# One issue in GpSimd's queue two operations later: the third sum of w_o blocks

## The chip, the cores and the metric

The kernel runs on one core of a Trainium2 chip. The metric is device time in microseconds of one execution. Every comparison is made against runs of the kernel before on the same chip. TensorE is called PE, VectorE DVE, ScalarE ACT, GpSimd POOL or G, and SyncE, which issues most transfers, SP.

## The reference

One decoder layer on x of shape (1, 512, 1024) in float32:

```python
h = x @ w_in                       # q, six k/v streams, gates, GDN q/k/v, beta, decay, merge gates
y_a = nsa_attention(...) @ w_nsa_out   # 8 heads of 64: compressed, selected and window branches
y_b = gated_deltanet(...) @ w_gdn_out  # 4 heads of 128: conv, chunked WY form, gated RMS norm
mix = (sigmoid(gate_a) * y_a + sigmoid(gate_b) * y_b) @ w_o
x = layer_norm(alpha * x + mix)
x = layer_norm(alpha * x + conv_ffn(x))    # (silu(gate) * val) @ w_down, gate and val through a width-3 conv
```

The DeltaNet inverts, for each head and chunk, a lower triangular matrix I + m. The products with `w_o` and `w_down` are what the sums of weight blocks below are for.

## The kernel before, in words

Each float32 product is made of three PE products of rounded parts: a tile `raw` is loaded, `wh` is its rounded copy (line 467 on ACT, 469 on DVE or GpSimd) and `wl = raw - wh` (line 471, on DVE or GpSimd, as a table says for each tile). PE then multiplies wh with the high and the low part of the other operand (lines 481 and 483, out is `gps` in the input projection) and wl with the high part (484).

The two output products, with `w_o` and `w_down`, are done as a seven-product scheme on 2x2 blocks, which needs sums of weight blocks. Those sums are made in DRAM by transfers that GpSimd issues, some of them adding (`accum_op`). For `w_o` they are the eight transfers of `sums_o`, written into `osum[0]` to `osum[3]`; nothing reads the finished sums before the product with `w_o`, some 390 us into the kernel (line 1168):

```python
todo = [(0, o[0, :, 0], 0), (1, o[0, :, 1], 0), (0, o[0, :, 1], 1), (1, o[1, :, 1], 1), (2, osum[1], 0), (2, o[0, :, 0], 1),
        (3, osum[2], 0), (3, o[1, :, 0], 1)]
for to, src, add in todo:
    G.dma_start(out=osum[to], in_=src, **({"accum_op": OP.add} if add else {}))
```

So `osum[2]` is first copied from `osum[1]`, then w_o's block (0, 0) is added to it, and `osum[3]` is copied from it later.

The order of every engine's instructions is written out: the table QUEUES has for each engine the numbers of its instructions (in the order in which the program makes them) in the order in which they are to run, and `queues` chains them with order-only dependencies. In the row of the table for Pool, 104 to 111 are the eight transfers of `sums_o`; 109 is the sixth, the adding transfer into `osum[2]`.

The place of the change lies where the DeltaNet of the third head is inverted while attention heads and the input projection run on PE beside it. The names there:

- `z` (line 772, GpSimd): the start of the inverse, made from `xs`, a DVE recursion of small steps (769, 770).
- `at` (line 740, GpSimd): a mask on the chunk's q-k products. It is used later, in `gdn_out` (line 861).
- CAST `wh` (469) and `wl` (471) on GpSimd: the first half of an input-projection tile, which PE takes up after the tile in work.
- `ym` (line 787, DVE) and line 790 on PE: a step of the inverse, `gdn_inv`:

```python
        PE.matmul(py[:, c, :], m[:, c, :], half(z)[:, c], start=True, stop=True)          # 785
    V.tensor_tensor(ym, py, bc(C["m16"][:, None, 0:64], (128, TT, 64)), op=OP.mult)       # 787
    ...
        PE.matmul(pz[:, c, :], x[:, c, :], ym[:, c, :], start=True, stop=True)            # 790
```

- `kh` and `kl` (907, ACT; 909, DVE): the two parts of the keys of the second group, which the scores (1039, 1040 on PE) need; the mask and exponent of the scores are lines 1043 and 1045.
- 656 and 1072 are PE transposes, 1086 and 1092 products of attention.

Of the kernel before, what the change touches and what calls it, by code (L numbers as in the profile page):

```python
# [70 lines left out]
def layout(a):  # L71
# [251 lines left out]
760-763 756 765-766 753 768-769 772 771 773-774 770 767 764 775 777 776 778-788 790 789 792 791 794 793 796 795  # L323
797-798""",
    "Pool": """2 1 0 8 10 9 11-12 3 13 4-6 15 7 16-17 19 141 20-22 27-28 105 33 23 25 18 34 29 39 38 30-31 43 32 14 44 40 107 24 35
37 140 62 26 41 45 54 48 55 42 36 49 51 47 52 64 66 65 67 46 68 57 69 58 50 53 56 59 61 108 104 63 109 75 60 76 80 88
77 81 87 90 110 78 71 84 72-73 70 93 85 74 92 94 86 82 91 95 111 144 96-97 83 98-99 79 100 106 101-102 89 103 112-130
132 131 133-137 147 150 138-139 142-143 145 153 148 146 149 151-152 154-155 157 156 158-161 163 162 165 164 166-171""",
    "SP": """0-7 17 8-9 15 25 10 12 11 13-14 19 18 16 20-24 26-75 80 79 81-82 78 83 77 84-85 76 86-134 136-165 167 135 169 171
# [1239 lines left out]
```

## Time and profile before

| what | value |
|---|---|
| runs | 825.55, 825.56, 827.45 us; median 825.56 |
| profiled execution | 824.98 us, with a span of 823.2 us |
| mean granted TensorE clock | 0.994 |
| PE busy | 804.0 us of the span |
| GpSimd busy | 179.5 us of the span, 176 instructions |
| adding and plain `osum` loads from w_o | 6 of 1024 KB, median 9.1 us from issue to landing |

The page shows one execution. Busy times are sums over the span; the chain of work that ended last is followed back from the last instruction to what released it. Rows of the order of time have the start in us, the duration in us, the engine, the line, the operation, what is written and read, and in square brackets the idle time of the engine ahead of it with what ended that. An engine's instructions are in order, so a wait at the head of a queue holds all behind it. Issues of transfers are not counted as busy time of their engine, but they stand in the rows.

### The profile page before, as it was taken

The page shows a single profiled execution, that of the slowest core. Times are in us where ns is not written, and L with a number is a line of the kernel's source. Part 1 is how long each engine was busy: PE and PEld are TensorE (multiplying, and loading weights), DVE is VectorE, ACT ScalarE, POOL GpSimd, SP SyncE. Part 2 cuts the span into 40 slices and gives each one's busy share as a digit, 9 for nine tenths or more (in the row PEclk, how much of TensorE's full clock was granted, in tenths as well). Part 3 has the DMA queues.
Part 4 walks back from the last instruction along what each step waited for, and adds up shares of the span by engine and source line. Part 5 has one row for each costly group of instructions (what it writes and reads, how often), then busy time and mean ns, then how long its engine had stood idle before and what let it go on. Part 6 is the DMA issues. An engine that isn't in the chain of part 4 may idle for free.

```text
span 823.2 us, 11781 instructions
## 1 busy us (share of the span) xinstructions
PE 804.0 (98%) x4138; PEld 672.5 (82%) x4138; DVE 602.7 (73%) x1339; ACT 409.0 (50%) x912; POOL 179.5 (22%) x176
## 2 busy tenths in 40 slices
PE   8999999999899999999999999999999999999996
PEld 8788888787788888888787898888888888878884
DVE  5667689979768965646568956667685666787888
ACT  4453577774477764513244333443443434555641
POOL 0344834032255201142200111111121201200000
PEclk9999999999899999999999999999999999999999
DMA  8327180013532923433447487376236393466774
GB/s 281 106 81 279 64 266 29 26 53 120 111 103 81 211 68 90 128 111 119 128 180 238 145 158 227 102 168 162 93 106 240 88 238 95 139 199 177 221 229 149
DMA packets 43978, 119.57 MB, mean 145 GB/s; under 512 B 3472, under 2 KB 4624, under 8 KB 43664
## 3 DMA queue, kind: packets, MB, share of 16 engines
q1 hardware_dynamic: 32144, 87.37, 33.0%
q0 software_dynamic: 11776, 31.46, 16.5%
q8 instruction: 32, 0.52, 0.3%
q14 instruction: 26, 0.21, 0.1%
HBM read 116.72 MB, written 33.55 MB: 183 GB/s over the span
## 4 chain that ended last, share of the span: by engine, by line
PE 81%; DVE 10%; DMA 5%; ACT 2%; issue 2%; SPq 0%; POOL 0%; DVEq 0%; ACTq 0%; POOLq 0%
PE pu L483 9%; PE pu L481 9%; PE pu L484 9%; PE gps L481 9%; PE gps L483 8%; PE gps L484 8%; PE pout L1086 2%; PE pz L1449 2%; PE px L1449 2%; PE aps L1072 2%; PE pm L481 2%; PE pm L483 2%; PE pm L484 2%; DVE wl L1385 2%; PE dps L656 1%
## 5 line engine op out<-in xcount | busy, mean ns | idle before, releaser
L471 DVE TENSOR_TENSOR wl<-raw,wh 128x512 fp32r<-128x512 f32 x146 | 106.4, 735 | 73.3 <-ACT wh L467 40.9
L467 ACT ACTIVATE wh<-raw 128x512 fp32r<-128x512 f32 x126 | 78.9, 629 | 138.6 <-PE pu L483 91.4
L484 PE MATMUL pu<-mh,wl 128*128 128x512 f32 (+1 forms) x384 | 129.9, 372 | 0.2 <-DVE wl L471 0.2
L481 PE MATMUL pu<-mh,wh 128*128 128x512 f32 (+1 forms) x384 | 129.8, 372 | 0.0
L483 PE MATMUL pu<-ml,wh 128*128 128x512 f32 (+1 forms) x384 | 129.6, 372 | 0.0
L481 PE MATMUL gps<-xh,wh 128*128 128x512 f32 x320 | 123.9, 400 | 2.4 <-ACT mt L1118 1.5
L483 PE MATMUL gps<-xl,wh 128*128 128x512 f32 x320 | 123.8, 398 | 0.0
L484 PE MATMUL gps<-xh,wl 128*128 128x512 f32 x320 | 123.0, 398 | 0.0
L484 PEld LDWEIGHTS pu<-mh,wl 128*128 128x128 f32 x384 | 71.3, 188 | 13.4 <-DVE wl L471 0.6
L481 PEld LDWEIGHTS pu<-mh,wh 128*128 128x128 f32 x384 | 71.0, 188 | 12.6
L483 PEld LDWEIGHTS pu<-ml,wh 128*128 128x128 f32 x384 | 71.0, 188 | 12.6
L1407 DVE SCALAR_TENSOR_TENSOR fa<-pu,fcw,fa 128x511 f32<-128x511 f32 (+1 forms) x88 | 65.0, 745 | 18.9 <-ACT fa L1404 18.3
L1413 POOL TENSOR_TENSOR fth<-fth,fa 128x512 f32<-128x512 f32 x22 | 31.2, 1427 | 196.9 <-DVE fth L1412 193.9
L481 PEld LDWEIGHTS gps<-xh,wh 128*128 128x128 f32 x320 | 60.3, 189 | 13.4 <-issue 2.8
L484 PEld LDWEIGHTS gps<-xh,wl 128*128 128x128 f32 x320 | 60.1, 189 | 10.9 <-POOL wl L471 0.2
L483 PEld LDWEIGHTS gps<-xl,wh 128*128 128x128 f32 x320 | 60.4, 189 | 10.6
L1384 ACT ACTIVATE wh<-raw 128x512 fp32r<-128x512 f32 x67 | 39.9, 625 | 36.3 <-DMA raw<-wsum 10.6
L1385 DVE TENSOR_TENSOR wl<-raw,wh 128x512 fp32r<-128x512 f32 x67 | 44.3, 691 | 14.5 <-ACT wh L1384 14.2
L1404 ACT ACTIVATE fa<-pu,fcw 128x512 f32<-128x512 f32 x44 | 29.5, 681 | 30.9 <-PE pu L484 29.4
L471 POOL TENSOR_TENSOR wl<-raw,wh 128x512 fp32r<-128x512 f32 x30 | 40.0, 1336 | 13.5 <-ACT wh L467 7.1
L522 POOL TENSOR_TENSOR rs<-rs,minus_half 128x1 f32<-128x1 f32 x8 | 7.6, 949 | 154.4 <-DVE rs L1243 102.1
L1045 ACT ACTIVATE sc<-sc,mn 128x384 f32<-128x384 f32 (+2 forms) x64 | 35.6, 558 | 9.3 <-DVE mn L1043 8.9
(365 smaller groups left out, 1706.3 us busy)
## 6 DMA issues: line engine op xcount, KB each, us to landing
raw<-in_up SPq DMA_DIRECT2D x44, 512.0 KB, 3.7
raw<-in_wT SPq DMA_DIRECT2D x40, 512.0 KB, 3.6
wsum<-in_down POOLq DMA_DIRECT2D x6, 2816.0 KB, 22.1
raw<-wsum SPq DMA_DIRECT2D x20, 512.0 KB, 3.9
raw<-in_down SPq DMA_DIRECT2D x15, 512.0 KB, 4.1
osum<-in_wo POOLq DMA_DIRECT2D x6, 1024.0 KB, 9.1
wsum<-wsum POOLq DMA_DIRECT2D x2, 2816.0 KB, 14.0
raw<-in_wm SPq DMA_DIRECT2D x8, 512.0 KB, 3.6
```

Of the source, the lines that this page charges most:

```text
L467: A.activation(wh, r, AF.Copy)
L471: eng.tensor_tensor(wl, r, wh.bitcast(F32), op=OP.subtract)
L481: i = PE.matmul(ps, wh[k], mh_(k), start=(k == 0), stop=False)
L483: PE.matmul(ps, wh[k], ml_(k), start=False, stop=False)
L484: PE.matmul(ps, wl[k], mh_(k), start=False, stop=(k == n - 1))
L1045: A.activation(s[:, i, :n], s[:, i, :n], AF.Exp, scale=-1.0, bias=mn[:, 0, i:i + 1], accum_out=mn[:, 1, i:i + 1])
L1384: A.activation(hi, raw[:, i], AF.Copy)
L1385: V.tensor_tensor(lo, raw[:, i], hi.bitcast(F32), op=OP.subtract)
L1404: A.activation(acc, ps, AF.Copy, scale=w[:, 2:3])
L1407: V.scalar_tensor_tensor(acc[:, n:], ps[:, :S - n], w[:, i:i + 1], acc[:, n:], op0=OP.mult, op1=OP.add)
L1413: G.tensor_tensor(th, th, g[1], op=OP.mult)
L1449: m = PE.matmul(ps, a[x][:, j, ts], w[y], start=first and i == 0, stop=last and i == 2, skip_group_check=True)
```

## The change

In the row of the table for Pool the number 109 moves two places back, behind 75 and 60, to the end of that row's old 63 109 75 60:

```diff
@@ "Pool" @@
-... 50 53 56 59 61 108 104 63 109 75 60 76 80 88
+... 50 53 56 59 61 108 104 63 75 60 109 76 80 88
```

On GpSimd, after the start of the inverse `z` (63), the CAST of the projection tile (75) and the mask `at` (60) now come ahead of the adding transfer into `osum[2]` (109), and the subtraction `wl` (76) follows that transfer. The difference on GpSimd, at its 74th to 82nd row:

```order
 L500 DMA osum_104<-in_wo 512x1x512
 L772 TENSOR_TENSOR z<-xs,cst 128x512
-L500 DMA osum_106<-in_wo 512x1x512
 L469 CAST wh<-raw 128x512
 L740 TENSOR_TENSOR at<-at,cst 128x512
+L500 DMA osum_106<-in_wo 512x1x512
 L471 TENSOR_TENSOR wl<-raw,wh 128x512
 L717 TENSOR_TENSOR grh<-cst,gdh 128x512
```

Only the transfer's issue has moved (osum_106 is `osum[2]`); CAST and `at` have nothing between `z` and them any more, and `wl` has the issue ahead of it.

DVE's order is the same in both. At this place it has, with what each waits for, the second half of the keys' low part for one product, then a projection tile's subtraction ahead of `ym`:

```order
L770 TENSOR_TENSOR xs<-xs,tmp 128x4 [waits DVE_49]
L909 TENSOR_TENSOR kl<-gps,kh 64x512 [waits PE_49,Activation_49]
L909 TENSOR_TENSOR kl<-gps,kh 64x512
L471 TENSOR_TENSOR wl<-raw,wh 128x512 [waits DMAHW4_49]
L787 TENSOR_TENSOR ym<-dps,cst 128x256 [waits PE_49]
L909 TENSOR_TENSOR kl<-gps,kh 64x512 [waits Activation_49]
```

Nothing moved here. The subtraction of line 471 stands ahead of `ym` before and after.

PE's order is the same in both too. Line 790 stands behind the transposes of the scores and waits for `ym`:

```order
L785 MATMUL dps<-z,m 128x64 [waits Activation_49]
L785 MATMUL dps<-z,m 128x64 x3
L656 MATMUL aps<-ident,cs 128x128
L1039 MATMUL aps<-kh,q_2451 128x2x128 [waits Activation_49]
L1086 MATMUL pout<-ptl,vcat 128x256
L1072 MATMUL aps<-ident,sc 128x128 [waits PE_49]
L1072 MATMUL aps<-ident,sc 128x128 x3
L790 MATMUL dps<-ym,x 128x64 [waits DVE_49,Activation_49]
```

Nothing moved here either; the orders of ACT and SP are the same as well.

More of the change, by code (lines that the diff above doesn't have):

```diff
@@ L325 @@
     "Pool": """2 1 0 8 10 9 11-12 3 13 4-6 15 7 16-17 19 141 20-22 27-28 105 33 23 25 18 34 29 39 38 30-31 43 32 14 44 40 107 24 35
-37 140 62 26 41 45 54 48 55 42 36 49 51 47 52 64 66 65 67 46 68 57 69 58 50 53 56 59 61 108 104 63 109 75 60 76 80 88
+37 140 62 26 41 45 54 48 55 42 36 49 51 47 52 64 66 65 67 46 68 57 69 58 50 53 56 59 61 108 104 63 75 60 109 76 80 88
 77 81 87 90 110 78 71 84 72-73 70 93 85 74 92 94 86 82 91 95 111 144 96-97 83 98-99 79 100 106 101-102 89 103 112-130
```

## The prediction

> **What bounds the kernel now.** I read the page first, for the engine that is full.
>
> ```profile
> PE 804.0 (98%) x4138; PEld 672.5 (82%) x4138; DVE 602.7 (73%) x1339; ACT 409.0 (50%) x912; POOL 179.5 (22%) x176
> PEclk9999999999899999999999999999999999999999
> ```
>
> TensorE (PE) is busy for 98% of the span, so the kernel is as long as PE's work plus PE's few stops. GpSimd (POOL), on which the change acts, is busy for 22%; it matters only where PE waits for something that POOL holds up. The second row has one slice out of forty with a lower granted clock, the eleventh (206 to 226 us). The moved transfer is issued in that slice, so next I read the chain of work that ended last, there (start, us, what).
>
> ```profile
> 211.69 0.68 DVE kl L909
> 212.38 0.03 issue
> 212.41 4.17 DVE wl L471
> 216.58 0.34 DVE ym L787
> 216.92 0.14 issue
> 217.06 1.94 PE dps L790 x8
> ```
>
> The chain leaves PE for one VectorE (DVE) instruction of 4.17 us: line 471's subtraction for a weight tile, on 128x512 elements. PE doesn't wait for that tile. It waits for `ym`, which stands behind it in DVE's queue. Next the list of waits, and the same place cut into stretches (length; then PE, PEld, DVE, ACT, POOL busy; granted clock; DMA).
>
> ```profile
> PE dps L790 <- DVE ym L787: 2.5, 1, 2.5
> 211.50:214.60 3.10, 2.98 (x25) 2.55 (x23) 3.05 (x3) 2.78 (x7) 3.10 (x5) 1.00 0.31 19
> 214.60:217.06 2.46, 0.00 (x2) 0.03 (x1) 2.43 (x3) 0.63 (x2) 1.42 (x2) 0.78 1.04 174
> 217.06:222.85 5.79, 5.79 (x18) 5.02 (x19) 3.63 (x15) 0.88 (x4) 0.00 (x0) 0.50 0.54 101
> 222.85:226.00 3.15, 3.15 (x47) 2.45 (x46) 1.55 (x7) 2.00 (x8) 0.00 (x0) 1.00 0.00 0
> ```
>
> This is PE's longest stop, 2.46 us, and it is paid for twice: behind it PE works 5.79 us at a granted clock of 0.50. So why did a subtraction take 4.17 us? GpSimd's instructions in order of time at that place:
>
> ```profile
> 210.75 1.05 POOL L772 TENSOR_TENSOR z<-xs,cst 128x512 f32<-128x512 f32 x1 [9.30 <-DVE xs L770]
> 211.75 1.20 POOL L500 DMA_DIRECT2D osum<-in_wo  x1
> 212.41 1.16 POOL L469 CAST wh<-raw 128x512 fp32r<-128x512 f32 x1
> 212.98 1.82 POOL L740 TENSOR_TENSOR at<-at,cst 128x512 f32<-128x512 f32 x1
> 214.21 1.81 POOL L471 TENSOR_TENSOR wl<-raw,wh 128x512 fp32r<-128x512 f32 x1
> ```
>
> and the same three forms without a transfer ahead of them:
>
> ```profile
> 164.38 1.27 POOL L471 TENSOR_TENSOR wl<-raw,wh 128x512 fp32r<-128x512 f32 x1
> 165.61 1.27 POOL L740 TENSOR_TENSOR at<-at,cst 128x512 f32<-128x512 f32 x1
> 166.83 0.61 POOL L469 CAST wh<-raw 128x512 fp32r<-128x512 f32 x1
> ```
>
> Undisturbed, each starts 0.04 us before its forerunner ends. Behind the transfer's issue each starts 0.54 to 0.59 us before that end and lasts about 0.55 us longer, as if a part of GpSimd were late by the issue and stayed late. DVE's subtraction starts at 212.41 together with GpSimd's CAST and ends 0.56 us after GpSimd's last piece (214.21 + 1.81 = 216.02). So it did nothing until GpSimd was through. Such waiting is found elsewhere, but for one GpSimd instruction at a time:
>
> ```profile
> 87.54 1.28 POOL L740 TENSOR_TENSOR at<-at,cst 128x512 f32<-128x512 f32 x1
> 88.28 1.09 DVE L652 SCALAR_TENSOR_TENSOR kq<-th,acc 128x512 f32<-128x512 f32 x1 [2.95 <-ACT th L645]
> 88.89 1.62 POOL L471 TENSOR_TENSOR wl<-raw,wh 128x512 fp32r<-128x512 f32 x1
> 64.09 1.27 POOL L748 TENSOR_TENSOR lo<-m,cst 128x512 f32<-128x512 f32 x1 [2.88 <-DVE m L738]
> 64.52 0.86 DVE L675 TENSOR_SCALAR ss<-ss 128x4 f32<-128x4 f32 x1
> 65.30 1.24 POOL L510 DMA_DIRECT2D wsum<-in_down  x1
> 102.93 1.23 POOL L500 DMA_DIRECT2D osum<-in_wo  x1
> 103.74 0.69 DVE L471 TENSOR_TENSOR wl<-raw,wh 128x512 fp32r<-128x512 f32 x1
> ```
>
> At 88 us DVE comes 0.54 us before `at` ends (88.82) and is done at 89.37, 0.55 us behind it; the next GpSimd piece pays. At 64 us GpSimd's next piece is a transfer's issue, and DVE is done 0.02 us behind `lo`. At 103 us the subtraction of our form runs in its plain 0.69 us inside the issue of an adding transfer. So DVE gets in between two GpSimd computations that don't overlap, and an issue doesn't hold it up.
>
> **The change part by part.** Nothing is added or taken away; the other four queues keep their order.
>
> 1. CAST and `at` come first. z ends at 211.80; with the rows from 164 us CAST runs 211.76 to 212.37 and `at` 212.33 to 213.60, without the stagger. Whether their inputs are there so early has no row of its own; they would wait only if a tile were freed later than 211.76, and then DVE, arriving at 212.41, would go first, which is no worse for it. DVE's arrival hangs on `kl` (211.69 + 0.68) and doesn't move.
>
> 2. The issue of the adding transfer stands behind `at`: 213.57 instead of 211.75, 1.82 us later. Its own cost to GpSimd stays 1.20 us.
>
> 3. GpSimd's `wl`, now behind the issue, ends at 213.57 + 1.20 + about 1.27, that is 216.0, as before (216.02). Nothing on PE's side gets later by it.
>
> 4. DVE waits for `at` alone: 213.60 + 0.55 = 214.15 instead of 216.58. Then `ym` (0.34 on the chain) and 0.14 of issue: PE can begin line 790 at 214.63. The work ahead of it on PE ends at 214.60:
>
> ```profile
> 212.42 1.00 PE L785 MATMUL dps<-z,m 128*128 128x64 f32 x8
> 214.00 0.60 PE L1072 MATMUL aps<-ident,sc 128*128 128x128 f32 x4
> ```
>
> So 217.06 - 214.63 = 2.43 us of the 2.46 go. If DVE went even before `at`, no more than the remaining 0.03 could be gained.
>
> 5. The half clock. The first row above is eight products of 64 columns in 1.00 us; line 790's eight took 1.94 at half the clock. If the clock stays, 5.79 us of full PE work become 2.90, so this part is worth between 0 (the spell stays) and 2.90. I take 2.8: the idle ahead of it shrinks from 2.46 to 0.03 us, and the 1.5 us stop below left no mark in the clock row. The 0.1 is for line 1040, which needs both `kl` pieces: they would be ready at about 214.5 + 1.4 = 215.9 and PE comes there at about 216.0, so there is hardly any room.
>
> 6. What is late next: PE itself. Behind 225 us it stops for at least 1 us at one place only, and the stretches are full:
>
> ```profile
> PE gps L481 <- ACT mt L1118: 1.5, 1, 1.5
> 225.00:250.00 25.00, 25.00 (x169) 21.09 (x168) 16.57 (x50) 19.01 (x60) 13.99 (x15) 1.00 0.26 87
> 250.00:300.00 50.00, 50.00 (x294) 42.93 (x292) 44.29 (x161) 36.76 (x102) 15.47 (x15) 1.00 0.61 131
> 480.00:733.00 253.00, 252.61 (x1153) 209.91 (x1152) 168.20 (x275) 107.83 (x187) 36.31 (x26) 1.00 0.57 156
> ```
>
> PE sets the pace to the end, and what it gains here moves everything behind it forward as one block.
>
> 7. The transfer's landing. The next in its line, the copy osum[3] from osum[2], waits for it at the head of GpSimd's queue, and GpSimd's further splits queue behind:
>
> ```profile
> DMA to landing us min/median/max: 6.2/7.8/9.4
> 233.89 0.71 POOL L500 DMA_DIRECT2D osum<-osum  x1
> ```
>
> With the longest of the three landings here, 9.4 us, it lands at 213.57 + 9.4 = 223.0. The copy comes up at 233.89 - 5.2 = 228.7. The cover is 5.7 us, so I cost the lateness at nothing; each us beyond that would hold GpSimd.
>
> Sum: 2.43 + 2.8 = 5.2 us off. The profiled execution took 824.98 us and would take 819.8; the median of the runs, 0.58 above it, goes from 825.56 to 820.4.
>
> **The rivals.**
>
> *The stop goes, the half clock stays.* From 211.5 to 217 us PE does mostly transposes and narrow products, and the idle time may only have completed a thin stretch. Then the spell runs from 216.0 (a mean clock of 0.78 over 2.46 us is 1.1 us at half, so it began 1.1 us ahead of 217.06) to 222.85 as before. By 222.85 PE would have done 1.37 us at full clock and 6.85 / 2 = 3.43 at half, together 4.80, against 2.90 before: 1.9 us gained, 823.7. Against it: the clock row shows no other dip, at the 1.5 us stop and at all the kernel's other transposes. [...]
>
> *DVE loses its turn anyway: no change.* If the transfer's issue held DVE up too, DVE would wait for CAST's followers to the last, 216.0 again, and PE would start at 217.06: 825.6. For it speaks a tiny DVE operation that ended with an issue:
>
> ```profile
> 105.88 1.09 POOL L510 DMA_DIRECT2D wsum<-in_down  x1
> 106.39 0.57 DVE L880 TENSOR_SCALAR so<-rn 128x4 f32<-128x4 f32 x1
> ```
>
> Against it, the row at 103.74, which has our form of subtraction.
>
> *Slower.* The same loss of turn, at a longer issue. One issue on this queue lasted 2.27 us:
>
> ```profile
> 264.89 2.27 POOL L510 DMA_DIRECT2D wsum<-in_down  x1
> ```
>
> Such an issue at 213.57, with DVE held to the end of the `wl` behind it, puts DVE's end 1.07 us later than now, at 217.65, and a longer stop could lengthen the half clock, by at most as much again (2.90 us): up to 829.5. It is a loss over 0.3% once PE's lost time grows by 2.5 us.
>
> **How the numbers follow.** Forecast 0.72; half clock stays 0.11; no change 0.12; slower 0.05. A measurement of this kernel tells about 0.3% (2.5 us) from no change, so the forecast is the only case that is faster by more: 0.74 with a little for half-way outcomes. The half-clock rival (0.2% faster) and the no-change one are "same": 0.20. Slower: 0.06. The range runs from the full 5.33 us against the profiled execution's own time (819.6, set to 819.5) to the half-clock rival, 823.7: 0.83 of the chances.
>
> **What would show it.** Right: DVE's `wl` at 212.4 us lasts about 1.7 us instead of 4.17; GpSimd's CAST takes 0.61 and `at` 1.27; the stagger moves to the `wl` behind the issue; the list of waits has no PE stop of 2.5 us at line 790; the clock row has no 8 in its eleventh slice, and PE's busy time falls by about 2.8 us. Wrong: a DVE subtraction that still ends at 216.6, a granted clock of 0.50 that stays, or a new stop of PE behind 225 us, at the copy of osum[3] above all.

## The result, and the profile after

The changed kernel took 821.16 us (median of 4, 820.75 to 822.81) against 825.92 (median of 4, 825.55 to 827.45): a ratio of 0.9943, 95% interval 0.9924 to 0.9962, 4.8 us less. The forecast was 820.4.

One thing has to be known to read the numbers below. Executions of the kernel before fall into two groups, one around 820 us and one around 825.5. In the first comparison all four were in the upper group. In the later runs it was 12 of 28, 23 of 35, 5 of 10 and 9 of 22. (Three executions of the kernel before, two of 1343 us at a granted clock of 0.557 and one of 4583 us, are left out of all numbers.) The changed kernel had none in the upper group in 16 executions. So the change takes away a loss of about 5 us that the kernel before has in some of its executions, and the median ratio depends on how many of those a comparison happens to catch. A second comparison gave 820.58 against 824.46, ratio 0.996 (0.994 to 0.9981).

The page after, first the busy times and the clock:

```profile
PE 802.4 (98%) x4138; PEld 670.2 (82%) x4138; DVE 600.2 (73%) x1339; ACT 409.1 (50%) x912; POOL 179.7 (22%) x176
PEclk9999999999999999999999999999999999999999
```

The dip in the clock row is gone. PE's busy time is only 1.6 us less, though the half clock alone had cost more (step 5 below). This execution was the slowest of its four (822.81), and busy time differs between executions of one kernel: 804.0 and 805.1 us in the two profiles of before with the wait, 802.4 and 801.8 in the two of the changed kernel. GpSimd's and DVE's order of time at the place of the change:

```profile
211.37 1.05 POOL L772 TENSOR_TENSOR z<-xs,cst 128x512 f32<-128x512 f32 x1 [9.24 <-DVE xs L770]
212.38 0.60 POOL L469 CAST wh<-raw 128x512 fp32r<-128x512 f32 x1
212.95 1.27 POOL L740 TENSOR_TENSOR at<-at,cst 128x512 f32<-128x512 f32 x1
214.16 1.19 POOL L500 DMA_DIRECT2D osum<-in_wo  x1
214.84 1.82 POOL L471 TENSOR_TENSOR wl<-raw,wh 128x512 fp32r<-128x512 f32 x1
213.03 1.73 DVE L471 TENSOR_TENSOR wl<-raw,wh 128x512 fp32r<-128x512 f32 x1
```

This execution is 0.62 us late already when `z` starts, so times are best counted from there. CAST and `at` have their plain 0.60 and 1.27 us, and the stagger has moved to the `wl` behind the issue. DVE's subtraction lasts 1.73 us instead of 4.17: it waits for `at` alone and is done 0.54 us behind it. The chain of work, and the stretches (columns as in the prediction):

```profile
214.28 0.39 PE aps L1039
214.67 0.12 PE pout L1086
214.79 0.44 PE aps L1072 x4
215.24 1.08 PE dps L790 x8
216.32 0.28 PE pout L1086
216.60 0.48 PE gps L481
```

```profile
211.50:214.60 3.10, 2.97 (x24) 2.69 (x23) 2.94 (x3) 2.76 (x8) 3.10 (x4) 1.00 0.00 0
214.60:217.06 2.46, 2.44 (x18) 1.90 (x17) 2.38 (x5) 1.26 (x3) 2.06 (x2) 1.00 0.38 26
217.06:222.85 5.79, 5.79 (x63) 4.49 (x61) 3.98 (x20) 3.60 (x14) 0.00 (x0) 1.00 0.97 174
```

DVE has left the chain; PE goes from line 1072 to 790 without a stop and at full clock. In the stretch that held 18 matmuls at half clock there are 63.

### The profile page after: what moved, and what is told of

Its sections match the earlier page's. It is cut to its first block, busy times and chain, and to the rows that moved or that the text cites. A ratio compares the mean times of both kernels' runs of the same rounds, so it can differ in the third digit from the quotient of the medians.

```text
span 820.8 us, 11781 instructions
## 1 busy us (share of the span) xinstructions
PE 802.4 (98%) x4138; PEld 670.2 (82%) x4138; DVE 600.2 (73%) x1339; ACT 409.1 (50%) x912; POOL 179.7 (22%) x176
## 4 chain that ended last, share of the span: by engine, by line
PE 79%; DVE 9%; DMA 7%; ACT 2%; issue 2%; SPq 0%; POOL 0%; DVEq 0%; ACTq 0%; POOLq 0%
PE pu L481 9%; PE pu L483 9%; PE pu L484 9%; PE gps L481 9%; PE gps L483 8%; PE gps L484 8%; DMA raw<-wsum 3%; PE pout L1086 2%; PE aps L1072 2%; DMA raw<-in_down 2%; DVE wl L1385 2%; PE pz L1449 2%; PE pm L483 2%; PE pm L481 2%; PE pm L484 2%
## 5 line engine op out<-in xcount | busy, mean ns | idle before, releaser
L471 DVE TENSOR_TENSOR wl<-raw,wh 128x512 fp32r<-128x512 f32 x146 | 103.9, 717 | 73.2 <-ACT wh L467 40.9
L1385 DVE TENSOR_TENSOR wl<-raw,wh 128x512 fp32r<-128x512 f32 x67 | 44.5, 691 | 15.8 <-ACT wh L1384 15.3
```

Source lines behind the costliest of these rows:

```text
L471: eng.tensor_tensor(wl, r, wh.bitcast(F32), op=OP.subtract)
L1385: V.tensor_tensor(lo, raw[:, i], hi.bitcast(F32), op=OP.subtract)
```

## The experiments

Theory 1, a guess of mine from the rows at 88.28, 103.74 and 212.41 us: a DVE operation with two inputs in SBUF can't start while GpSimd computes on SBUF; behind an issue GpSimd's computations overlap (there by 0.54 to 0.59 us), so it waits for the whole run of them. Theory 1a adds that it is a race: which of the two begins first decides. The rivals are named in the expectations. In the diffs only GpSimd's row is shown, unless another engine is named.

**Half the change.** The issue goes behind the CAST only.

```diff
-104 63 109 75 60 76 80 88
+104 63 75 109 60 76 80 88
```

> The adding transfer's issue one place later than before (behind the CAST, ahead of the mask at), half of the change. Times from z's start. Theory 1 (GpSimd computations behind an adding issue overlap, and a DVE subtraction of two SBUF tiles must wait until none is under way): DVE's wl comes 0.04 us after the CAST has ended and ahead of at, so it runs in 0.7 us instead of 4.17; no PE stop at line 790, clock row without a dip; kl is ready earlier than in the changed kernel, so the time is 820.4 to 821.2, ratio 0.994 or slightly lower than the changed kernel's. Theory 2 (the issue itself keeps DVE out until GpSimd's run behind it is over): the issue has begun when DVE comes, so wl lasts 3.6 to 4.2 us and the time is that of before, 825.6. Theory 3 (what counts is when the transfer's packets move, 1.8 us later in the changed kernel): here they move 0.6 us later, and at least two thirds of the loss stays, 824 or more.

Measured: 820.92 us median, but in two groups: 7 of 12 at 819.9 to 821.0, 5 at 823.5 to 826.3; ratio 0.9998 (0.997 to 1.0025). The first profile fell in the lower group:

```profile
211.81 0.60 POOL L469 CAST wh<-raw 128x512 fp32r<-128x512 f32 x1
212.36 1.20 POOL L500 DMA_DIRECT2D osum<-in_wo  x1
212.42 0.69 DVE L471 TENSOR_TENSOR wl<-raw,wh 128x512 fp32r<-128x512 f32 x1
```

Here theory 1 holds to the letter, wl 0.69 us. But the upper group wasn't foreseen, and the kernel before, on the same chip, had both groups too. So the same kernel was profiled once more.

> Another profile of the half change (the issue between CAST and at), which had 5 of 12 executions at 823.5 to 826.3. If its time is above 823: theory 1a expects that DVE came late enough (or the CAST ended late enough) for DVE to be kept out through at and wl, about 3.6 us, with a stop of about 2 us at line 790; if wl is short there, the slow group comes from something else, such as a spell of half clock without a stop. Below 823: as in its first profile, 0.7 us.

The second profile, of an execution of 823.14 us:

```profile
211.40 0.61 POOL L469 CAST wh<-raw 128x512 fp32r<-128x512 f32 x1
211.96 1.20 POOL L500 DMA_DIRECT2D osum<-in_wo  x1
212.07 4.15 DVE L471 TENSOR_TENSOR wl<-raw,wh 128x512 fp32r<-128x512 f32 x1
212.64 1.81 POOL L740 TENSOR_TENSOR at<-at,cst 128x512 f32<-128x512 f32 x1
213.87 1.79 POOL L471 TENSOR_TENSOR wl<-raw,wh 128x512 fp32r<-128x512 f32 x1
```

The same order of instructions gives 0.69 us in one execution and 4.15 in the other. DVE came 0.01 us behind the CAST's end the first time and 0.06 the second. The wait ends 0.56 us behind GpSimd's last piece (213.87 + 1.79 = 215.66), as it did before the change. This goes against theory 1 as I had put it: no computation is shown under way at 212.07, only the issue, and DVE was kept out all the same, longer than the 3.6 us that were expected. PE's stop at line 790 was 2.4 us.

**A shorter run behind the issue.** The issue stays; GpSimd's `wl` goes behind the next piece, which waits for PE.

```diff
-104 63 109 75 60 76 80 88
+104 63 109 75 60 80 76 88
```

> The issue stays where it was before; GpSimd's third piece behind it, wl, is put behind the next one (which waits until 228 us for PE), so that only the CAST and at follow the issue. Theory 1: DVE's wl lasts until 0.55 us behind at's end, 214.80 + 0.55 = 215.35 on the old clock, 2.9 us instead of 4.17; PE's stop at line 790 is 1.2 us instead of 2.46. If a stop of this length brings no half clock, the time is about 821.5 (ratio 0.995); if it does, about 824.4 (0.9985). Theories 2 and 3 (the issue itself, or the transfer's packets): nothing changes for DVE, 4.2 us and 825.6.

Measured: 822.2 us median, from 819.58 to 823.91, ratio 0.9989 (0.9962 to 1.0015). Its profile, of an execution of 823.88:

```profile
212.65 1.83 POOL L740 TENSOR_TENSOR at<-at,cst 128x512 f32<-128x512 f32 x1
212.09 2.95 DVE L471 TENSOR_TENSOR wl<-raw,wh 128x512 fp32r<-128x512 f32 x1
```

and in its list of waits:

```profile
PE dps L790 <- DVE ym L787: 1.2, 1, 1.2
```

DVE waits to the end of the shortened run: 212.65 + 1.83 + 0.56. The 2.9 and 1.2 us that were expected are there, so the run of GpSimd behind the issue sets the length of the wait. A spell of half clock followed here too (last section). Six of the ten executions were below 823, and none reached 825.

**Another operation first on DVE.** GpSimd as before; on DVE, `ym` and the second pair of `kl` go ahead of `wl`.

```diff
-484-485 497 432 486-487 520
+484-485 432 486-487 497 520
```

> GpSimd's order is that of before, with the issue ahead of CAST, at and wl; on DVE the subtraction wl goes behind ym and the second pair of kl. Theory 1 (only DVE operations with two SBUF inputs wait; ym and kl have one input in PSUM): ym starts at about 213.5 and takes 0.4 us in the middle of GpSimd's overlapping run, line 790 starts without a stop, wl comes at about 215.3 and ends at 216.6 as before; time 820.5 to 821.5, ratio 0.994 to 0.995. If GpSimd's run held up DVE as a whole, ym would be late as before and the time 825.6.

Measured: 821.47 us, one group, 820.48 to 822.49; ratio 1.0004 (0.9985 to 1.0022) against executions of before of both groups.

```profile
212.97 0.42 DVE L787 TENSOR_TENSOR ym<-dps,cst 128x256 f32<-128x256 f32 x1 [1.08 <-PE dps L785]
214.85 1.30 DVE L471 TENSOR_TENSOR wl<-raw,wh 128x512 fp32r<-128x512 f32 x1
```

GpSimd's staggered run goes on from 211.96 to 215.59 there, and `ym`, with one input in PSUM, takes its plain 0.42 us in it. Of the DVE operations there only the subtraction of two SBUF tiles waits: 1.30 us, against 0.69 at 103.74 us in the kernel before, while `ym` takes 0.42 and the two `kl` behind it 1.40 (1.38 for the first pair in the profile of before). The long stop was paid because `ym` stood behind it. A smaller price stays: the weight tile is late, PE's line 484 waits 0.33 us for it, and from the start of line 790 to that of 809 PE takes 7.01 us (213.95 to 220.96), against 5.97 in the 820.1 us profile of before that is shown further down. Two SBUF inputs aren't the whole condition, though, and theory 1 is too narrow there: in the prediction's own row at 64.52 us line 675, a TENSOR_SCALAR on one tile of 128x4, lasted 0.86 us until just behind GpSimd's `lo`, while the median of its eight is 0.16.

**Before and after once more, on another chip.**

> The kernel before, unchanged, with a profile of its own. The first comparison had its four executions at 825.5 to 827.5; on the chip of the half change it had 16 of 28 near 820 and 12 from 823.7 to 827.6. Theory 1a (a race): in the profile before, DVE's wl and GpSimd's CAST begin at the same 212.41 us, so which of them is first can change from execution to execution; where DVE is first, wl takes 0.7 us, there is no stop and no dip of the clock, and the execution is near 820.3; where the CAST is first, 4.2 us, a stop of 2.5 us with a half clock behind it, and 825.5 or more. So its executions fall in those two groups again, and its profile shows the wait that belongs to its time. Rival theory 4 (the groups come from the granted clock alone, the same stop in all of them): wl lasts 4.2 us in a fast execution too.

> The changed kernel, unchanged, on this chip. Theory 1a: DVE comes either just before at takes its turn or within it, and both do no harm (wl 0.7 or 1.7 us), so it has no executions of 825 or more: one group at 819.5 to 822.8, and the gain against before is the share of before's slow executions times 5.4 us. Theory 4: a half-clock spell comes by chance in thin PE work without a stop: then it has a second group near 824 (3.4 us of PE work lost in a 6.8 us spell, or 1.7 us in one of 3.4).

The kernel before: 35 executions spread from 818.17 to 821.87 (12) and from 823.65 to 827.44 (23), medians of the groups 819.7 and 825.4; ten more were five near 820 (819.57 to 820.96) and five from 823.35 to 825.62. The profile was of an execution of 1342.84 us and shows nothing on the question. The changed kernel: 12 executions from 819.87 to 821.66, no upper group. Its profile has the same 1.7 us wait as the first, with `at` from 212.04 to 213.30:

```profile
212.13 1.72 DVE L471 TENSOR_TENSOR wl<-raw,wh 128x512 fp32r<-128x512 f32 x1
```

**Two more profiles of the kernel before.**

> Another profile of the kernel before, to see one of its fast executions. If the time is below 823: theory 1a (a race between DVE's wl and GpSimd's CAST) expects DVE's wl to begin some hundredths of a us ahead of the CAST, to last 0.7 us, no stop at line 790 and no dip; theory 4 (the clock alone) expects the 4.2 us wait and the 2.5 us stop with the clock at 1.00. If it is above 823, the 4.2 us wait as in the first profile.

> A third profile of the kernel before, as about half of its executions were near 820 on the last two chips and none of those has been profiled. Below 823: theory 1a expects DVE's wl of 0.7 us, begun at most 0.1 us earlier against the CAST than in the slow profiles (0.00 and 0.01 us behind its start), no stop at line 790 and a clock of 1.00; theory 4 (the clock alone) expects the wait of 4.2 us and the stop to be there with the clock at 1.00. Above 823: the wait of 4.2 us again.

The first took 826.89 us, the second 820.1. GpSimd and DVE in the first, then in the second:

```profile
212.57 1.16 POOL L469 CAST wh<-raw 128x512 fp32r<-128x512 f32 x1
212.58 4.15 DVE L471 TENSOR_TENSOR wl<-raw,wh 128x512 fp32r<-128x512 f32 x1
```

```profile
212.26 0.69 DVE L471 TENSOR_TENSOR wl<-raw,wh 128x512 fp32r<-128x512 f32 x1
212.29 1.16 POOL L469 CAST wh<-raw 128x512 fp32r<-128x512 f32 x1
213.39 1.30 POOL L740 TENSOR_TENSOR at<-at,cst 128x512 f32<-128x512 f32 x1
```

and in the second the two stretches in which PE had stopped and then run at half clock in the first profile of before:

```profile
214.60:217.06 2.46, 2.46 (x16) 2.14 (x16) 2.25 (x9) 1.19 (x6) 1.32 (x2) 1.00 1.07 180
217.06:222.85 5.79, 5.79 (x67) 4.51 (x66) 3.50 (x16) 3.89 (x15) 0.34 (x1) 1.00 0.67 131
```

This is the race. Where DVE begins 0.03 us ahead of the CAST, it takes 0.69 us, PE doesn't stop and the clock stays full; where it begins 0.00 or 0.01 us behind it, it waits 4.2 us. That rests on one profile without the wait and two with it. In the one without it the stop and the spell are absent too, so the rival that the clock alone makes the groups falls. Where DVE is first, `at` isn't staggered either (1.30 us, begun 0.06 us ahead of the CAST's end).

Counted from the start of `z` (210.75 and 210.91 us in the two profiles with the wait, 210.63 in the one without), the CAST begins at 1.66 us in all three, while DVE comes at 1.66 and 1.67 with the wait and at 1.63 without. The half change shows nearly the same two values: counted from `z` (210.80 and 210.40), DVE came at 1.62 us where it was let in and at 1.67 where it was kept out, with the CAST over at 1.61 both times.

**A plain issue in the adding one's place.**

```diff
-61 108 104 63 109 75 60 76
+61 108 109 63 104 75 60 76
```

> At the place of the adding transfer's issue before stands another of the eight, a plain copy of a w_o block (104), and the adding one goes ahead of z. Such an issue took 0.74 to 0.79 us instead of 1.20, and a computation behind one (234.6 us) wasn't staggered. Theory 1 with the stagger from the adding issue alone: CAST and at keep their 0.61 and 1.27 us, DVE's wl takes 0.7 to 1.8 us, no stop: 820 to 821.5. If any issue staggers what follows it: the same 4.2 us and 2.5 us stop as before in part of the executions, 825.5.

Measured: 820.92 us, from 819.44 to 825.07; ratio 0.9971 (0.9947 to 0.9995). The profile, of an execution of 822.8:

```profile
211.83 0.73 POOL L500 DMA_DIRECT2D osum<-in_wo  x1
212.48 0.70 POOL L469 CAST wh<-raw 128x512 fp32r<-128x512 f32 x1
212.49 3.68 DVE L471 TENSOR_TENSOR wl<-raw,wh 128x512 fp32r<-128x512 f32 x1
```

The expectation of theory 1 fails. A plain issue lengthens the CAST by only 0.1 us, and DVE, 0.01 us behind the CAST, still loses every turn; PE stops for 2.0 us at line 790. A long stagger isn't needed. This profile is also a warning about times: an execution of 822.8 us can hide a lost turn, so a time below 823 by itself doesn't prove that DVE was let in.

**Two issues in a row ahead of the CAST.**

```diff
-104 63 109 75 60 76
+63 109 104 75 60 76
```

> GpSimd has two issues in a row where before had one: the adding transfer and behind it the plain one (104, which stood ahead of z), so that the CAST can't begin before about 212.9 on the old clock. Theory 1a: DVE's wl comes at 212.41 while no GpSimd computation is under way, is first in every execution and takes 0.7 us, although more staggering than ever follows; no stop, one group at 819.5 to 822.5. If issues harm by themselves, or by the stagger that they leave: 4 us and more for wl, and 825.5.

Measured: 820.54 us, one group, 819.42 to 822.25; ratio 0.9984 (0.9964 to 1.0005).

```profile
211.60 2.02 POOL L500 DMA_DIRECT2D osum<-in_wo  x2
212.28 0.69 DVE L471 TENSOR_TENSOR wl<-raw,wh 128x512 fp32r<-128x512 f32 x1
212.90 1.34 POOL L469 CAST wh<-raw 128x512 fp32r<-128x512 f32 x1
```

The CAST is 0.62 us behind DVE, and no execution is in an upper group, although the stagger (CAST 1.34 us) is the longest of all. In the kernel before and here, what decides is who comes first; the second profile of the half change is the case that this rule doesn't cover.

**The issue elsewhere: behind `wl`, or ahead of `z`.**

```diff
-104 63 109 75 60 76 80 88
+104 63 75 60 76 109 80 88      # behind wl
+104 109 63 75 60 76 80 88      # ahead of z
```

> The issue one place later than in the changed kernel, behind GpSimd's wl, so that CAST, at and wl run back to back without an issue among them, each starting 0.04 us before its forerunner ends. DVE comes at the start of at. Theory 1: it gets its turn at at's end (213.6 on the old clock, wl 1.7 us, no stop, 820 to 821.5), or, since at 168 us a DVE operation was passed over by one GpSimd piece that began 0.03 us early, at the end of GpSimd's wl (214.9 + 0.55 = 215.4, wl 3.0 us, a stop of 1.2 us, 821.5 to 824). It can't be passed over twice, so no execution of 825.5 or more.

> The adding transfer's issue goes ahead of z, some 5 us earlier than before, so that CAST, at and wl follow z without an issue. Theory 1: as with the issue behind wl, DVE gets its turn at at's end, wl 1.7 us, no stop, one group at 819.2 to 822. Theory 3 (a later movement of the packets is what helps): the packets move earlier, so the kernel is no faster than before, with executions of 825.5.

Measured: 820.44 us (819.25 to 821.45), ratio 0.9954 (0.9936 to 0.9973), and 821.18 us (819.52 to 822.21), ratio 0.9989 (0.9967 to 1.001); one group each. Behind `wl`:

```profile
212.04 1.26 POOL L740 TENSOR_TENSOR at<-at,cst 128x512 f32<-128x512 f32 x1
212.09 1.76 DVE L471 TENSOR_TENSOR wl<-raw,wh 128x512 fp32r<-128x512 f32 x1
213.27 1.72 POOL L471 TENSOR_TENSOR wl<-raw,wh 128x512 fp32r<-128x512 f32 x1
```

Without an issue ahead, DVE gets its turn at the end of `at`, although the next piece starts 0.03 us before that end. The overlap alone is no rule: at 168 us, in the expectation above, 0.03 us were enough to pass over a DVE operation of another form (line 1056, 1.68 us, done 0.21 us behind that GpSimd piece). Ahead of `z` DVE's wl lasts 1.76 us as well. There the packets move earlier instead of later, and the upper group is gone all the same, so theory 3 falls. Two versions ran beside the changed kernel (820.58): the issue behind `wl` with 820.44 and the plain issue with 820.92. Neither beats it by what can be measured; the others ran at other times and weren't compared with it.

## Why the prediction was right, by its own steps

1. *CAST and `at` without stagger*: 0.60 and 1.27 us, forecast 0.61 and 1.27.
2. *The issue 1.82 us later*: counted from `z`, 2.79 us instead of 1.00, that is 1.79.
3. *GpSimd's wl ends as before*: 5.29 us behind z's start, 5.27 before.
4. *DVE waits for `at` alone*: 1.73 us, forecast 1.74. Line 790 starts 3.87 us behind z's start, before 6.31: 2.44 us, forecast 2.43.
5. *The half clock* was mis-sized. From the start of line 790 to that of 809 it took 8.62 us before (217.06 to 225.68) and 6.18 after (215.24 to 221.42, rows below). That is 2.44 gained, forecast 2.8. Two things make up the 0.36 us. First `kl`, for which I had allowed 0.1 us: it was ready 5.16 us behind z's start (215.13 + 1.40), and the product ahead of line 1040 took 0.48 us on the chain instead of the 0.23 of its neighbours, so it cost about 0.25, that is 0.15 more. Second, work at half clock didn't take twice as long: the same products of 512 columns (line 483) took 0.43 us on the chain before and 0.23 after. Without a wait for `kl` and at full clock the way from 790 to 809 took 5.93 us in the first profile of the half change (214.45 to 220.38) and 5.97 in the 820.1 us profile of before (214.30 to 220.27), so the spell cost at most 2.69 us and not 2.90; that is the other 0.21.
6. *PE next*: the longest stop behind 225 us is still the 1.5 us one. But not everything moved forward as one block: in the profiled execution line 1285 began 4.3 us earlier than before (419.4 instead of 423.7), the first product into `pz` (line 1449) 3.6 earlier (733.3 instead of 736.9), and the span was 2.4 shorter. In the second profile of the changed kernel it was 5.0, 5.0 and 4.0. Why the end of the kernel gives some of the gain back is open.
7. *The landing*: at most 9.4 us again, so 223.6, against the copy at 229.65; a cover of 6.1 us, forecast 5.7.

```profile
DMA to landing us min/median/max: 6.5/8.2/9.4
```

```profile
229.65 0.71 POOL L500 DMA_DIRECT2D osum<-osum  x1
```

PE's rows for step 5, in order of time, before and after:

```profile
225.68 0.44 PE L809 MATMUL dps<-ym,x 32*32 32x32 f32 x16
221.42 0.44 PE L809 MATMUL dps<-ym,x 32*32 32x32 f32 x16
```

and a product of line 483 on the chain, before and after:

```profile
220.18 0.43 PE gps L483
217.20 0.23 PE gps L483
```

Steps 4 and 5 together make 4.9 us; the first comparison showed 4.8.

None of the rivals came true. The half clock stayed in neither profile of the changed kernel, DVE didn't lose its turn in any of its 16 executions, as far as the times tell, and nothing got slower.

The number owes something to luck. The forecast took the wait for what every execution of before pays, and all four of that comparison did pay it. In the second comparison, where 23 of 35 did, the median fell by 3.9 us instead of 4.8, and on the chip of the half change, where 12 of 28 did, the median of before was already 820.65: the forecast gain could not have shown in a median there.

What the prediction lacked is the race. It quoted the two starts, 212.41 for DVE and for the CAST, and treated DVE as the second; the 4.17 us were taken for what the order of instructions does, while it does so only in a part of the executions. And its sentence that an issue doesn't hold DVE up holds for 103.74 us and not for the second profile of the half change. In the changed kernel DVE comes 0.08 us after the start of `at`, close to the CAST's end too, but there it waited for one computation (1.73 us), not for three (4.17).

Still open: what GpSimd does during an issue that keeps DVE out, and from when. The half change kept DVE out at 0.06 us behind the CAST's end and 0.11 us into the issue, and let it in at 0.01 and 0.06. Open too is where the stagger comes from: that a part of GpSimd is late by the issue was a guess of mine, and no run here shows GpSimd's parts singly.

## What to carry to other kernels

When a DVE operation on two SBUF tiles lasts several times its plain time, compare its end with the end of GpSimd's run: here, in every profile in which the subtraction waited, it ended 0.54 to 0.56 us behind the GpSimd computation that it had waited for, at a plain time of 0.69. Look for a transfer's issue directly ahead of a run of GpSimd computations at a place where PE waits for DVE: here one cost about 5 us in part of the executions (12 of 28, 23 of 35), though two in a row cost nothing that could be measured. Look too at what stands behind the waiting operation on DVE, since moving that ahead (`ym` here) took away the stop of 2.5 us without touching GpSimd. Where two starts in a profile lie within a few hundredths of a microsecond (here 0.00 and 0.01 us behind, 0.03 ahead), look at more than one execution before believing either outcome.

## What the runs showed of the hardware that was not expected

In the profiles taken here the half-clock spells have two lengths, about 6.8 and 3.4 us. Ten microseconds from 214 us, in the first profile of before, the second profile of the half change, and the shorter run (the last number but two is the granted clock):

```profile
214.00:224.00 10.00, 7.54 (x45) 6.25 (x44) 7.00 (x18) 2.52 (x8) 2.02 (x2) 0.66 0.60 104
```

```profile
214.00:224.00 10.00, 7.57 (x50) 6.09 (x49) 7.29 (x21) 3.20 (x12) 1.67 (x2) 0.83 0.64 107
```

```profile
214.00:224.00 10.00, 8.77 (x70) 6.90 (x69) 6.90 (x23) 4.24 (x15) 0.48 (x1) 0.83 0.59 104
```

Within a spell the granted clock was 0.50 (217.06 to 222.85 us in the first profile of before), so a mean of 0.66 over ten microseconds is 6.8 us at half, one of 0.83 is 3.4. The half change with the wait had a stop of 2.4 us and a spell of 3.4, the plain issue one of 2.0 and 3.4 (0.83 too); the kernel before had one of 2.46 and a spell of 6.8, and in its profile of 826.89 us one of 2.43 and 6.8 (0.66). In the shorter run a stop of 1.2 us was enough for 3.4, while behind the 1.5 us stop at line 1118, near 400 us, the clock of the stretches from 350 to 400 and from 400 to 450 us is 1.00 in the profiles of the first before, the changed kernel, the first half change, the shorter run and `ym` first. The page's clock row can't show this: in the shorter run, the plain issue and the second profile of the half change it has no 8 in its eleventh slice, though each has a spell there (3.4 us at half in a slice of 20.5 leave a mean of 0.92, a 9), so the prediction's argument from that row was weaker than it looked. So the length of the stop alone doesn't set the price; what starts a spell and what sets its length, no run here shows.
